# A two-layer MLP on one core: the second product in fp16 parts with ranges found on the way, three of four relu-squares split over two engines, and W2 read earlier

## The chip, the core and the metric

The kernel runs on one core of a Trainium2 chip. TensorE (PE in the profile, its weight loads PEld) multiplies, VectorE (DVE) and ScalarE (ACT) work element by element, GpSimd (POOL) does a few powers, and SyncE (SP) issues the DMA transfers from one queue, in order. The metric is the device time of one execution in microseconds; the median of several is compared.

## The reference

One layer of a hybrid backbone over 128 context tokens and 2048 latent tokens, with 1024 features. Each token stream goes through a mixer (gated DeltaNet beside a gated MLP over chunks), which the change doesn't touch, and then through this:

```python
h = rmsnorm(x, norm_ffn_l) * (1.0 + sc2) + sh2
x = x + ga2 * (jnp.square(jax.nn.relu(h @ w_ff1_l)) @ w_ff2_l)
...
y_prompt = rmsnorm(x, norm_final)
y_sample = rmsnorm(y, norm_final)
```

`w_ff1` is 1024 x 4096, `w_ff2` 4096 x 1024, all in fp32. Below, W1 and W2 are these two, z is the relu-square between them, and the gate is `ga2`. Latent and context tokens have gates and modulation of their own.

## The kernel before, in words

The program first makes the modulation, then the input projections with the mixer's first half, then the scans with the output projection, and last the MLP. Some 2500 us, of which the MLP is the second half.

**Parts.** An fp32 operand is multiplied as a high part and a low part: `mm3` (lines 309 to 315) makes three matmuls for each 128-wide piece of the contraction, high by high, high by low and low by high (lines 313, 314, 315). In the mixer and in the first MLP product the parts are fp16 (`split16x4`, line 1686: ScalarE writes the scaled high part, line 1694, VectorE the low part, line 1695). The scale is a power of two that is found from sums of squares of the operand: `powers` (line 223) turns a column of 128 maxima with a PE transpose (line 226), takes the largest on VectorE, spreads it over the partitions with a small PE product (line 231) and keeps the exponent. In the second MLP product the parts are `fp32r` (`split4`, line 1698: a ScalarE cast, line 1702, and a VectorE subtract, which has the line of `add`, 1684).

**First MLP product, 1201 to 1849 us.** The 2048 latent tokens times W1, in two halves of 1024 tokens and 16 pairs of 128-column blocks: 32 units (`Unit`). Each unit is a 2 x 2 block product done with seven products in place of eight (the numbers 1, 5, 6, 7, 3, 2, 4 are its steps, in that order), each of 12 matmuls of 512 columns. The moving operand (`hop`) is the normalised input in fp16 parts, the stationary one (`w`) sums or differences of W1 blocks, prepared six steps ahead. A unit's results are the four blocks of z: p (named for its first content, step 7), c12 (step 3), c11 (step 2) and c21 (step 4). VectorE adds up what PSUM holds (`add_scaled`, line 1707) and makes the relu-square in one instruction (`rl2`, line 1669); for c11 alone ScalarE does relu and square (lines 1803, 1804). Each block goes to DRAM (`z_d`, line 1765), and so do the sums s1 = c12 + p and s2 = s1 - c11 (line 1768), which the second product needs. The loop over the 224 steps (line 2116) sets the order in which all this is recorded, with other work between: `h2_steps` (the input of the second token half, first half of the loop), and `context_steps` (the same product for the 128 context tokens, second half). Also there, in the second half: the 16 differences of W2 blocks that the second product needs first, `sums_load(0, k)` at every sixth step and `sums(0, k)` four steps later (lines 2118 to 2122): two tiles r are loaded, VectorE subtracts them (line 1684), SP stores the result in `t_d`. A scheduling layer then moves instructions within each engine's queue by its own estimate of when their inputs are there.

**Second MLP product, 1849 to 2507 us.** Again seven products (1, 5, 6, 7, 3, 4, 2), each over eight or nine pairs of token tiles u and four quarters q of the contraction; one (product, u, q) is 12 matmuls of 512 columns. The stationary operand is z or a sum of its blocks (`s_load` reads it from DRAM five places ahead, `s_build` at line 1943 splits it three places ahead), the moving one the W2 blocks of the product (`t_build`, line 1885, four 128-row pairs to a `hop` buffer, four buffers to a product). `outcome` adds the PSUM results up, and `final` multiplies by the gate, adds the residual and normalises. Further differences of W2 are made during products 1, 5 and 6, and rows of the modulation during product 6.

**Buffers.** A pool of 49 tiles of 2 KB a partition (`wp`, line 170) holds all operands under way in the MLP: raw loads, split operands, blocks of z. A load waits until the tile it goes into has been given up. PSUM has eight banks (`bank`).

## Time and profile before

| | us |
|---|---|
| runs shown | 2512.78, 2520.37, 2521.24 |
| median | 2520.37 |
| the profiled execution's own time | 2515.55 |
| its span, first to last instruction | 2513.8 |
| first MLP product | 1201 to 1849 |
| second MLP product | 1849 to 2507 |

The clock granted to TensorE was 0.992 of full on average. A line of the profile such as `L313 PE MATMUL f<-hop,zH 128*128 128x512 f32 x944 | 367.3, 389 | 0.4 ...` reads: source line, engine, operation, output from inputs by the program's names, shape and type, count, then the busy time in us and the mean duration of one in ns, then the engine's idle time just ahead of these and what ended it. Matmuls overlap, so their pace is read from start to start and not from their durations. `SPq` is the queue of DMA issues.

### The profile page before, as it was taken

The numbers are of one execution on the slowest core, as the hardware profiler recorded it, in microseconds if no ns is written. First come the engines' busy times: TensorE is split into PE (matmuls) and PEld (weight loads), VectorE is DVE, ScalarE is ACT, GpSimd is POOL, SyncE is SP. The second block draws the span as 40 slices with busy tenths as digits, with TensorE's granted clock in tenths as the row PEclk, the third lists the DMA queues.
The fourth block names the chain that finished last, engine by engine and source line by source line (L and its number), as shares of the span: only waits on it lengthen the run. The fifth ranks groups of instructions, "written<-read, shape, count | busy, mean of one in ns | idle before, by whom it ended". The sixth has DMA issues, their size and how long they took to land.

```text
span 2513.8 us, 44098 instructions
## 1 busy us (share of the span) xinstructions
PE 2462.8 (98%) x15188; PEld 1666.3 (66%) x15188; DVE 1883.3 (75%) x3898; ACT 1339.5 (53%) x3257; POOL 236.9 (9%) x429
## 2 busy tenths in 40 slices
PE   8999999999999999999999999999999999999998
PEld 4666667666666787888444444444468888888887
DVE  4868886877778888986688988778765557685775
ACT  3756764566666667763456655445344323243442
POOL 3112222111111211110000000000000000000000
PEclk9999999999999999999999999999999999999999
DMA  8767755665656656774666778767689879776773
GB/s 293 227 179 216 221 164 174 201 202 183 205 186 194 203 169 216 250 239 134 218 205 205 232 233 283 242 206 221 188 282 315 312 251 334 239 263 200 236 255 108
DMA packets 482791, 558.23 MB, mean 222 GB/s; under 512 B 38068, under 2 KB 285148, under 8 KB 482566
## 3 DMA queue, kind: packets, MB, share of 16 engines
q1 hardware_dynamic: 482566, 555.41, 69.0%
q8 instruction: 119, 1.95, 0.3%
q14 instruction: 106, 0.87, 0.1%
HBM read 399.19 MB, written 156.08 MB: 221 GB/s over the span
## 4 chain that ended last, share of the span: by engine, by line
PE 78%; DVE 9%; DMA 6%; ACT 3%; issue 2%; SPq 1%; POOL 1%; POOLq 0%; DVEq 0%; ACTq 0%
PE f L315 15%; PE f L313 15%; PE f L314 15%; PE pj L313 5%; PE pj L314 5%; PE pj L315 5%; PE pd L1136 4%; PE pm L313 2%; PE pm L314 2%; PE pm L315 2%; DMA QK<-qk_d 2%; PE pt L683 1%; DMA r<-in_w_ff_dram 1%; DMA raw<-in_w_mod_dram 1%; PE pt L642 1%
## 5 line engine op out<-in xcount | busy, mean ns | idle before, releaser
L315 PE MATMUL f<-hop,zL 128*128 128x512 f32 (+1 forms) x976 | 376.2, 386 | 1.3 <-DVE zL L1684 1.2
L313 PE MATMUL f<-hop,zH 128*128 128x512 f32 (+1 forms) x976 | 376.4, 386 | 0.4 <-ACT zH L1702 0.4
L314 PE MATMUL f<-hop,zH 128*128 128x512 f32 (+1 forms) x976 | 376.1, 386 | 0.0
L313 PE MATMUL f<-hop,w 128*128 128x512 f16 x896 | 340.3, 381 | 3.1 <-ACT p L1786 2.3
L314 PE MATMUL f<-hop,w 128*128 128x512 f16 x896 | 341.1, 381 | 0.0
L315 PE MATMUL f<-hop,w 128*128 128x512 f16 x896 | 340.2, 381 | 0.0
L1702 ACT CAST zH<-zraw 128x512 fp32r<-128x512 f32 x240 | 146.4, 620 | 299.5 <-DMA zraw<-s_d 89.1
L314 PEld LDWEIGHTS <-w 128*128 128x128 f16 x1536 | 151.3, 99 | 148.8 <-issue 10.9
L313 PEld LDWEIGHTS <-w 128*128 128x128 f16 x1536 | 151.1, 98 | 146.9 <-issue 4.4
L315 PEld LDWEIGHTS <-w 128*128 128x128 f16 x1536 | 151.2, 98 | 146.5 <-issue 5.7
L1684 DVE TENSOR_TENSOR zL<-zraw,zH 128x512 fp32r<-128x512 f32 x240 | 163.2, 688 | 73.1 <-ACT zH L1702 58.5
L315 PEld LDWEIGHTS f<-hop,zL 128*128 128x128 f32 x976 | 183.4, 188 | 38.9 <-DVE zL L1684 2.2
L313 PEld LDWEIGHTS f<-hop,zH 128*128 128x128 f32 x976 | 183.4, 188 | 37.8 <-ACT zH L1702 0.9
L314 PEld LDWEIGHTS f<-hop,zH 128*128 128x128 f32 x976 | 183.4, 188 | 36.9 <-issue 0.2
L313 PE MATMUL pj<-kH,w 128*128 128x386 f16 (+2 forms) x568 | 180.3, 321 | 6.0 <-ACT w L205 3.3
L314 PE MATMUL pj<-kL,w 128*128 128x386 f16 (+2 forms) x568 | 181.2, 322 | 0.0
L315 PE MATMUL pj<-kH,w 128*128 128x386 f16 (+2 forms) x568 | 180.4, 321 | 0.0
L181 POOL TENSOR_TENSOR r<-rsq,nhalf 128x1 f32<-128x1 f32 (+1 forms) x37 | 27.7, 749 | 1368.2 <-DVE rsq L180 1368.2
L1694 ACT ACTIVATE w<-s,scales 128x512 f16<-128x512 f32 x96 | 68.7, 719 | 163.2 <-DVE s L1684 162.9
L1684 DVE TENSOR_TENSOR r<-r,r 128x512 f32<-128x512 f32 x64 | 44.2, 691 | 96.3 <-DMA r<-in_w_ff_dram 96.3
L629 DVE SCALAR_TENSOR_TENSOR cv<-pj,vec,cv 128x384 f32<-128x384 f32 (+2 forms) x142 | 83.1, 589 | 26.7 <-ACT cv L627 25.5
L313 PE MATMUL pj<-w,hrow 128*128 128x512 f16 x256 | 97.1, 379 | 0.1
(453 smaller groups left out, 5494.3 us busy)
## 6 DMA issues: line engine op xcount, KB each, us to landing
raw<-in_w_ff_dram SPq DMA_DIRECT2D x256, 256.0 KB
zraw<-z_d SPq DMA_DIRECT2D x212, 256.0 KB
z_d<-c SPq DMA_DIRECT2D x96, 256.0 KB
r<-in_w_ff_dram SPq DMA_DIRECT2D x96, 256.0 KB
zraw<-s_d SPq DMA_DIRECT2D x96, 256.0 KB
raw<-in_w_mod_dram SPq DMA_DIRECT2D x80, 256.0 KB
s_d<-s SPq DMA_DIRECT2D x64, 256.0 KB
t_d<-r SPq DMA_DIRECT2D x64, 256.0 KB
```

The source lines that it names most:

```text
L181: G.tensor_tensor(out=out, in0=t[:np_, :n], in1=nhalf[:np_, :n], op=ALU.pow)
L313: T.matmul(ps, lh, rh, start=first and i == 0, stop=False, skip_group_check=more)
L314: T.matmul(ps, lh, rl, start=False, stop=False, skip_group_check=more)
L315: T.matmul(ps, ll, rh, start=False, stop=last and i == n - 1, skip_group_check=more)
L629: V.scalar_tensor_tensor(out=cv, in0=ps[:, w : w + ncol - 2], scalar=convw[:, w, j : j + 1], in1=cv, op0=ALU.mult, op1=ALU.add)
L642: T.transpose(pq[:, i * P : (i + 1) * P], u["x2"][i], ident)
L683: T.matmul(ps[:, i * P : (i + 1) * P], kTt[:, i * P : (i + 1) * P], rhs[i], start=True, stop=True)
L1136: T.matmul(p[:, h, :], lhs[:, h, :], rhs[:, h, :], start=True, stop=True)
L1684: V.tensor_tensor(out=out, in0=a, in1=b, op=op)
L1694: A.activation(h, src, AF.Copy, scale=scale)
L1702: A.copy(h, src)
```

## The change

- z and W2 are split in fp16 parts, each scaled by a power of two; the product of the two scales is taken out again where the gate is multiplied in. Operand tiles take half the room: one pool tile in place of two for a piece of z, and two `hop` buffers in place of four for a product's W2.
- z's power comes from column sums of z itself (the squares of the relu), which ScalarE adds up while it squares (`accum_out`). So p, c12 and c21 become a max with 0 on VectorE and a square on ScalarE; c11 and the context tokens' squares get the sum too. `z_range` finds the power from the sums, for the first token half in the loop's second half, and for the others early in the second product.
- W2's power comes from squares of all of W2, which ScalarE makes (in place, 64 tiles). So the loop loads all four tiles of a step of W2, from step 11 on at every eleventh, and nine steps later subtracts two of them and squares all four. `w2_range` is recorded fifteen steps ahead of the first split of W2.
- A few of the steps of `h2_steps` move by one place.

Names in the rows below: p, c and s are the blocks and sums above, f is PSUM, w a split operand, r a tile of W2, `stats` the tile of column sums.

VectorE in one unit's steps 7 and 3, the program before:

```order
L1707 SCALAR_TENSOR_TENSOR c_21845<-f,scales,x 128x512 [waits DMAHW1_49,PE_49]
L1669 SCALAR_TENSOR_TENSOR p_21817<-p_21817 128x512 [waits DVE_49]
L1669 SCALAR_TENSOR_TENSOR c_21845<-c_21845 128x512 [waits DVE_49]
L1684 TENSOR_TENSOR s_21849<-c_21845,p_21817 128x512 [waits DVE_49]
L206 SCALAR_TENSOR_TENSOR w_21855<-raw,scales,w_21855 128x512 [waits DMAHW3_49,Activation_49]
L1695 SCALAR_TENSOR_TENSOR w_21861<-s,scales,w_21861 128x512 [waits Activation_49]
```

and with the change:

```order
L1737 SCALAR_TENSOR_TENSOR c_22079<-f,scales,x 128x512 [waits DMAHW2_49,PE_49]
L1681 TENSOR_SCALAR p_22050<-p_22050 128x512 [waits DVE_49]
L1681 TENSOR_SCALAR c_22079<-c_22079 128x512 [waits DVE_49]
L1722 TENSOR_TENSOR s_22084<-c_22079,p_22050 128x512 [waits Activation_49]
L1722 TENSOR_TENSOR t_22095<-r_21837,r_21835 128x512
L206 SCALAR_TENSOR_TENSOR w_22090<-raw,scales,w_22090 128x512 [waits DMAHW4_49,Activation_49]
```

The two relu-squares became two max, and the sum behind them now waits for ScalarE.

The SP queue around one read of W2 in the loop's second half, before:

```order
L1848 DMA z_d<-z_21586 256x1x128 [waits DMAHW2_49]
L1879 DMA r_21629<-in_w_ff_dram 128x512 [waits DMAHW3_49,PE_49]
L1879 DMA r_21631<-in_w_ff_dram 128x512 [waits DMAHW4_49]
L1905 DMA t_4_d<-r_21629 128x512 [waits DMAHW5_49,DVE_49]
L1765 DMA z_d<-p_21620 128x4x128 [waits DMAHW6_49,DVE_49]
```

and with the change, first on SP, then on ScalarE at the same place of the program:

```order
L1795 DMA z_d<-c_22118 128x4x128 [waits DMAHW3_49,Activation_49]
L187 DMA raw<-in_w_ff_dram 128x512 [waits DMAHW4_49,PE_49]
L1798 DMA s_d<-s_22122 128x4x128 [waits DMAHW5_49,DVE_49]
L1909 DMA r_22155<-in_w_ff_dram 128x512 [waits DMAHW6_49]
L1909 DMA r_22157<-in_w_ff_dram 128x512 [waits DMAHW7_49]
L1909 DMA r_22159<-in_w_ff_dram 128x512 [waits DMAHW0_49,PE_49]
L1909 DMA r_22161<-in_w_ff_dram 128x512 [waits DMAHW1_49,PE_49]
L1795 DMA z_d<-c_22145 128x4x128 [waits DMAHW2_49,Activation_49]
```

```order
L1677 ACTIVATE c_22145,stats<-c_22145 128x512 [waits DVE_49]
L1732 ACTIVATE w_22171<-raw,scales 128x512
L1805 ACTIVATE x<-f,scales 128x512 [waits DMAHW0_49,PE_49]
L1876 ACTIVATE z_22190,stats<-f 128x512 [waits PE_49]
L205 ACTIVATE w_22202<-raw,scales 128x512 [waits DMAHW3_49]
L1707 ACTIVATE r_22159,stats<-r_22159 128x512 [waits DMAHW0_49]
L1732 ACTIVATE w_22207<-raw,scales 128x512 [waits DMAHW7_49,DMAHW6_49]
L1809 ACTIVATE p_22223<-f,scales 128x512 [waits PE_49]
L1707 ACTIVATE r_22161,stats<-r_22161 128x512 [waits DMAHW1_49]
```

Before, the store of the difference stood directly behind its loads on SP. Now it stands far behind them, and so does the subtract on VectorE; but the squares of the two tiles that aren't subtracted stand on ScalarE about two steps behind the loads, in front of a copy out of PSUM (p).

The diff, cut to its core:

```diff
-    def rl2(out, src):
-        V.scalar_tensor_tensor(out=out, in0=src, scalar=0.0, in1=src, op0=ALU.max, op1=ALU.mult)
+    def square_z(c, g, n):
+        A.activation(c, c, AF.Square, accum_out=z_sums[g][:, n : n + 1])
+    def rl2(c, g, n):
+        V.tensor_scalar(out=c, in0=c, scalar1=0.0, scalar2=None, op0=ALU.max)
+        square_z(c, g, n)
+    def z_range(gs):
+        n, sl = len(gs), slice(gs[0], gs[-1] + 1)
+        top = smp.tile([P, 8], F32, tag="topc", name="topz", bufs=1)[:, 0:n]
+        for i, g in enumerate(gs):
+            V.tensor_reduce(out=top[:, i : i + 1], in_=z_sums[g], axis=mybir.AxisListType.X, op=ALU.max)
+        V.tensor_scalar_mul(top, top, 4.0)
+        powers(z_power[:, sl], z_under[:, sl], top, n, bank)
+        if 2 in gs:
+            V.tensor_scalar_mul(y_under, z_under, w2_under)
+    def w2_range():
+        top = smp.tile([P, 8], F32, tag="topc", name="topw", bufs=1)[:, 0:1]
+        V.tensor_reduce(out=top, in_=w2_sums, axis=mybir.AxisListType.X, op=ALU.max)
+        four_sum_power(w2_power, w2_under, top, bank, True)
+    def w2_loads(k):
+        return [fetch(rows2(k, h, n)) for h in (0, 1) for n in (0, 1)]
+    def w2_first(k, r):
+        d = w512("t5")
+        add(d, r[1], r[0], ALU.subtract)
+        store(out=t_d[5, k], in_=d)
+        for i in range(4):
+            A.activation(r[i], r[i], AF.Square, accum_out=w2_sums[:, 4 * k + i : 4 * k + i + 1])
...
     def t_build(raw, k):
-        if k % 4 == 0:
+        if k % 8 == 0:
             tcount.append(0)
-            moved.append(hop_tile(F32R, (len(tcount) - 1) % 5 < 2))
-        t = moved[-1][:, k % 4]
-        A.copy(t[:, 0, :], raw)
-        add(t[:, 1, :], raw, f32(t)[:, 0, :], ALU.subtract)
+            moved.append(hop_tile(F16, (len(tcount) - 1) % 5 < 2))
+        t = moved[-1][:, k % 8 // 4, k % 4]
+        raw = as4(raw)
+        A.activation(t[:, 0], raw, AF.Copy, scale=w2_power)
+        V.scalar_tensor_tensor(out=t[:, 1], in0=raw, scalar=w2_power, in1=t[:, 0], op0=ALU.mult, op1=ALU.subtract)
...
-    def s_build(raws, rest):
+    def s_build(raws, rest, u):
         if rest:
             add(raws[0], raws[0], raws[1], rest[0])
-        return split4(raws[0], "z")
+        g = token_group(u)
+        return split16x4(raws[0], z_power[:, g : g + 1])
...
-        add(y[n], y[n], ga[n], ALU.mult)
+        gated(y[n], y[n], ga[n], t)
...
-        if p > half + 7 and p % 6 == 0 and len(begun_sums) < NK:
+        if p >= 8 and p % 11 == 0 and len(begun_sums) < NK:
             begun_sums.append(p)
-            first_sums.append((p, len(begun_sums) - 1, sums_load(0, len(begun_sums) - 1)))
-        while first_sums and p >= first_sums[0][0] + 4:
-            sums(0, *first_sums.pop(0)[1:])
+            first_sums.append((p, len(begun_sums) - 1, w2_loads(len(begun_sums) - 1)))
+        while first_sums and p >= first_sums[0][0] + 9:
+            w2_first(*first_sums.pop(0)[1:])
+        if p == last - 12:
+            w2_range()
+        if p == half + 8:
+            z_range([0])
...
         us = products[n][1]
+        if m == 3:
+            z_range([1, 2])
```

More of the change, by code (lines that the diff above doesn't have):

```diff
@@ L1665, in hybrid_step @@
     wst.close()
-    def rl2(out, src):
-        V.scalar_tensor_tensor(out=out, in0=src, scalar=0.0, in1=src, op0=ALU.max, op1=ALU.mult)
+    stats = wp.tile([P, 512], F32, tag="w", name="stats")
+    z_sums = [stats[:, 0:64], stats[:, 64:128], stats[:, 128:136]]
+    w2_sums = stats[:, 192:256]
+    V.memset(stats[:, 256:384], 1.0)
+    phase["ones"] = stats[:, 256:384]
+    w2_power, w2_under = stats[:, 384:385], stats[:, 385:386]
+    z_power, z_under = stats[:, 386:389], stats[:, 389:392]
+    y_under = stats[:, 392:395]
+    def square_z(c, g, n):
[24 more added lines that the diff above has]
+            A.activation(r[i], r[i], AF.Square, accum_out=w2_sums[:, 4 * k + i : 4 * k + i + 1])
     hops["B"] = ctx.enter_context(tc.tile_pool(name="hopB", bufs=1, reuse_waits="tile"))
@@ L1695, in split16x4 @@
             V.scalar_tensor_tensor(out=lo, in0=src, scalar=scale, in1=h, op0=ALU.mult, op1=ALU.subtract)
-        return h, lo
-    def split4(src, name="w"):
-        h = wp.tile([P, 4, P], F32R, tag="w", name=name + "H")
-        lo = wp.tile([P, 4, P], F32R, tag="w", name=name + "L")
-        A.copy(h, src)
-        add(lo, src, f32(h), ALU.subtract)
         return h, lo
@@ L1788, in step @@
                 add(z, z, t["p5"])
-                rl2(z, z)
+                rl2(z, self.g, 4 * self.jp)
                 self.out(1, 1, z)
@@ L1794, in step @@
                 add_scaled(c, ps[5], t["x"])
-                rl2(c, c)
+                rl2(c, self.g, 4 * self.jp + 1)
                 self.out(0, 1, c)
@@ L1803, in step @@
                 A.activation(c, ps[1], AF.Relu, scale=mlp_under)
-                A.activation(c, c, AF.Square)
+                square_z(c, self.g, 4 * self.jp + 2)
                 self.out(0, 0, c)
@@ L1812, in step @@
                 add_scaled(c, ps[7], t["x"])
-                rl2(c, c)
+                rl2(c, self.g, 4 * self.jp + 3)
                 self.out(1, 0, c)
@@ L1902, in sums @@
     def sums(i, k, r):
-        if i < 2:
+        if i == 1:
             add(r[0], r[1], r[0], ALU.subtract)
-            store(out=t_d[7 if i else 5, k], in_=r[0])
+            store(out=t_d[7, k], in_=r[0])
         elif i == 5:
@@ L1958, in hybrid_step, with gated, half_out @@
     rows = {}
-    def half_out(y, n, x, ga, ss):
-        add(y[n], y[n], ga[n], ALU.mult)
+    def gated(out, y, ga, t):
+        g = 2 if t == 0 else 0 if t > 8 else 1
+        V.scalar_tensor_tensor(out=out, in0=y, scalar=y_under[:, g : g + 1], in1=ga, op0=ALU.mult, op1=ALU.mult)
+    def half_out(t, y, n, x, ga, ss):
+        gated(y[n], y[n], ga[n], t)
         add(y[n], y[n], x[n])
@@ L1970, in final @@
         ss = smp.tile([P, 2], F32, tag="ss2", name="ss2")
-        half_out(y, 1, x, ga, ss)
+        half_out(t, y, 1, x, ga, ss)
         def rest():
-            half_out(y, 0, x, ga, ss)
+            half_out(t, y, 0, x, ga, ss)
             r = smp.tile([P, 1], F32, tag="r", name="r")
@@ L1989, in final_last @@
         r = smp.tile([P, 1], F32, tag="r", name="r")
-        add(y[1], y[1], ga[1], ALU.mult)
+        gated(y[1], y[1], ga[1], t)
         add(y[1], y[1], x[1])
@@ L1993, in final_last @@
         add(y[1], y[1], nf[1], ALU.mult)
-        add(y[0], y[0], ga[0], ALU.mult)
+        gated(y[0], y[0], ga[0], t)
         add(y[0], y[0], x[0])
@@ L1999, in part @@
             c = slice(256 * h, 256 * h + 256)
-            add(x[0][:, c], ps[:, 0:256], ga[0][:, c], ALU.mult)
+            gated(x[0][:, c], ps[:, 0:256], ga[0][:, c], t)
             add(y[0][:, c], x[0][:, c], y[0][:, c])
@@ L2107, in hybrid_step @@
         p = 10 + 19 * j // 2
-        later += [(p + (-4, 0, 1, 2, 4, 5)[k] if k < 6 else p + 2 * k - 6, st[k]) for k in range(len(st))]
+        later += [(p + (-4, 0, 1, 2, 5, 6)[k] if k < 6 else p + 2 * k - 5, st[k]) for k in range(len(st))]
     later.sort(key=lambda e: e[0])
```

8 lines of the change are left out of this document (4 added, 4 removed).

## The prediction

> **What bounds the kernel now.** I read the page first, then the windows by stage, then the timeline of single matmuls, then the groups and the waits of the two MLP products. The page's first part has TensorE (PE) busy for nearly all of the span:
>
> ```profile
> PE 2462.8 (98%) x15188; PEld 1666.3 (66%) x15188; DVE 1883.3 (75%) x3898; ACT 1339.5 (53%) x3257; POOL 236.9 (9%) x429
> ```
>
> Busy says little of pace, so here is the busy time by stretch. The first MLP product runs from 1201 to 1849 us, the second from 1849 to 2507 us. Columns: stretch, its length, then busy time and instruction count of PE, weight loads, VectorE, ScalarE, GpSimd, then granted clock, DMA share, GB/s.
>
> ```profile
> 1200.00:1500.00 300.00, 296.84 (x1403) 139.20 (x1402) 246.16 (x403) 170.94 (x325) 8.18 (x9) 0.99 0.71 219
> 1700.00:1800.00 100.00, 98.36 (x462) 45.13 (x461) 79.59 (x123) 51.44 (x82) 0.00 (x0) 1.00 0.68 209
> 1900.00:2000.00 100.00, 100.00 (x443) 82.81 (x442) 51.03 (x78) 38.68 (x68) 0.00 (x0) 1.00 0.88 309
> ```
>
> At the same clock of 1.00 the first product issues 462 matmuls in 100 us, small gaps included, the second only 443, with none. The timeline of PE shows why: first two rows of the first product, then two of the second.
>
> ```profile
> 1700.18 0.38 PE L313 MATMUL f<-hop,w 128*128 128x512 f16 x1
> ...
> 1711.84 0.38 PE L313 MATMUL f<-hop,w 128*128 128x512 f16 x1
> ```
>
> ```profile
> 1929.69 0.39 PE L313 MATMUL f<-hop,zH 128*128 128x512 f32 x1
> ...
> 1935.81 0.39 PE L313 MATMUL f<-hop,zH 128*128 128x512 f32 x1
> ```
>
> Between the first pair lie 54 starts: 11.66 us / 54 = 215.9 ns from start to start. Between the second lie 27: 6.12 / 27 = 226.7 ns. The second product is bound by PE at 226.7 ns a matmul, the first at 215.9 ns plus a few stalls. The groups carry the counts:
>
> ```profile
> L313 PE MATMUL f<-hop,zH 128*128 128x512 f32 x944 | 367.3, 389 | 0.4 <-ACT zH L1702 0.4
> L313 PEld LDWEIGHTS f<-hop,zH 128*128 128x128 f32 x976 | 183.4, 188 | 37.8 <-ACT zH L1702 0.9 <-issue 0.2
> L313 PEld LDWEIGHTS <-w 128*128 128x128 f16 x149 | 14.6, 98 | 17.4
> L1684 DVE TENSOR_TENSOR zL<-zraw,zH 128x512 fp32r<-128x512 f32 x240 | 163.2, 688 | 73.1 <-ACT zH L1702 58.5 <-PE f L314 4.6 <-issue 2.7
> L1702 ACT CAST zH<-zraw 128x512 fp32r<-128x512 f32 x240 | 146.4, 620 | 299.5 <-DMA zraw<-s_d 89.1 <-DVE zraw L1684 84.5 <-DMA zraw<-z_d 71.6
> L1695 DVE SCALAR_TENSOR_TENSOR w<-raw,scales,w 128x512 f16<-128x512 f32 x14 | 10.2, 743 | 0.0
> L1694 ACT ACTIVATE w<-raw,scales 128x512 f16<-128x512 f32 x14 | 9.9, 714 | 0.0
> L341 DVE TENSOR_SCALAR macc<-mraw,scond 128x512 f32<-128x512 f32 x4 | 1.7, 479 | 0.0
> L1669 DVE SCALAR_TENSOR_TENSOR c<-c 128x512 f32<-128x512 f32 x12 | 8.2, 686 | 0.1
> ```
>
> **The second product in fp16.** Its 3 x 944 = 2832 full matmuls (three lines of equal count) go from fp32r to fp16. No row of this kernel has an fp16 stationary z. Bounds: nothing gained (226.7 ns stays) or the whole step to 215.9 ns. I take the second, since the first product's row has the same shape, the same three-part sum and the same 98 ns weight load that the change will have in place of 188 ns. 2832 x 10.8 ns = **30.6 us**; the 96 half-width matmuls add some 0.5 us at most. Sum **-31 us**, all on the path, as PE has no gap in that stage that would swallow it.
>
> What pays for it: each of 240 + 112 splits becomes a scaled copy and a subtract. ScalarE +0.1 us each (714 against 620 ns), VectorE +0.055 us (743 against 688): 35 and 19 us over 658 us. Cover: VectorE was busy 51 of 100 us and ScalarE 39 there; in the fullest 20 us below VectorE has 18.3, which the extra 0.055 in 0.69 and the faster pace bring near 20. With no cover, 19 us would be lost.
>
> **The relu-squares.** Three of four per unit (32 units) were one VectorE instruction of 686 ns; now they are a max (nearest rows: 479 ns single-source, 686 at worst; I take 479) and a square on ScalarE with a column sum. That pair's price on ScalarE is in the timeline of the same form, L972, 0.61 us from start to start:
>
> ```profile
> 1360.27 0.62 ACT L972 ACTIVATE junk<-x 128x512 f32<-128x512 f32 x1
> 1360.79 0.19 ACT L972 ACTIVATION_READ_ACCUMULATOR junk<-x 128x1 f32 x1
> 1360.88 0.62 ACT L972 ACTIVATE junk<-x 128x512 f32<-128x512 f32 x1
> ```
>
> A new wait appears: s1 = c12 + z22 stands on VectorE right behind the two max, and now waits for two squares on ScalarE. Free ScalarE: 0.6 to 1.3 us; I take 1.0. Queued behind it on VectorE are the low halves of the next weights and the c21 sum, for which PE waits. Per unit of 300 / 16 = 18.7 us VectorE had 18% = 3.4 us idle (first window); it gains 3 x 0.2 us, and pays 1.0 of wait and 0.69 x 7/11 = 0.4 for the W2 difference that now falls in this half: +0.8 us, inside the 3.4. ScalarE: 57% busy; 3 x 0.61 plus 4 x 0.61 x 7/11 for W2 is 3.4 us of 18.7: 75%. I take **+2 us** of small stalls for it (0 if all fit).
>
> **W2 earlier.** In the second half of the first product, waits and the traces of one stall:
>
> ```profile
> DVE r L1684 <- DMA r<-in_w_ff_dram: 53.0, 13, 5.6
> ACT w L1694 <- DVE s L1684: 158.0, 55, 8.2
> PE f L1845 <- ACT r L1840: 3.2, 3, 1.9
> PE f L313 <- ACT p L1786: 2.3, 1, 2.3
> ```
>
> ```profile
> SPq L1905 <- DVE r L1684: 41.4, 10, 8.2
> ```
>
> ```profile
> 1652.72 0.69 DVE L1684 TENSOR_TENSOR r<-r,r 128x512 f32<-128x512 f32 x1 [5.23 <-DMA r<-in_w_ff_dram]
> ```
>
> ```profile
> 1654.71 0.72 ACT L1694 ACTIVATE w<-s,scales 128x512 f16<-128x512 f32 x1 [7.39 <-DVE s L1684]
> 1655.34 0.67 ACT L1786 ACTIVATE p<-f,scales 128x512 f32<-128x512 f32 x1
> ```
>
> ```profile
> 1653.40 0.38 PE L315 MATMUL f<-hop,w 128*128 128x512 f16 x1
> 1656.06 0.38 PE L313 MATMUL f<-hop,w 128*128 128x512 f16 x1 [2.29 <-ACT p L1786]
> ...
> 1656.94 0.63 PE L314 MATMUL f<-hop,w 128*128 128x512 f16 x1
> ...
> 1660.33 0.38 PE L313 MATMUL f<-w,w 128*128 128x512 f16 x1
> ```
>
> VectorE waits 5.2 us for a W2 tile that came late; ScalarE waits 7.4 us for a weight sum queued behind it; a PSUM copy (p) queued behind that holds PE for 2.3 us. After the gap eight matmuls take 3.39 us (1656.94 to 1660.33) in place of 1.73: the stall costs 2.3 + 1.7. The SP queue stood too, on the store of that difference. The change puts the subtract a unit or more behind its load, so PE's 2.3 and 3.2 us with two slow tails (1.7 shown, the other estimated alike) should go: 5.5 + 3.4 = **-9 us**. What is late next: two of the four squares of W2 stand on ScalarE only two steps (5 to 6 us) behind their load, with PSUM copies behind them, so some of that wait moves to ScalarE. I leave **+3 us** of it.
>
> The clock row can be set against the Trainium skill, page "TensorE: Matmul & The Clock Gate", section "HAM oscillation": gaps under about 3.4 us should not slow the clock. The trace disagrees, as a gap of 2.66 us did. By the rule the credit would be 5.5 us and the total some 3 us higher; the row decides.
>
> **The range tests.** Three power computations add a transpose and a small product on PE, amid other matmuls. The same helper's row (min, median, max ns):
>
> ```profile
> L226 PE MATMUL pm<-ident,topw x2: 270/272/273, 797.8 to 807.4; 128*1 128x128 f32 x2
> ```
>
> Three such pieces apiece, overlapped or not: 1 to 2.4 us together; **+1 us**. The stores' wait on SP lengthens by the square; SP gains the 41.4 us above, so nothing is added. The gate's multiply gets a scalar (743 against 688 ns), off PE's path but for two half tiles at the end: 0.1 us.
>
> **DMA in the second product.** Same bytes in less time:
>
> ```profile
> 1860.00:1880.00 20.00, 18.32 (x80) 14.57 (x79) 8.91 (x13) 5.93 (x10) 0.00 (x0) 1.00 1.02 357
> 1880.00:1900.00 20.00, 20.00 (x90) 16.53 (x89) 10.21 (x15) 6.08 (x10) 0.00 (x0) 1.00 0.98 338
> 1900.00:1920.00 20.00, 20.00 (x90) 16.57 (x89) 9.20 (x15) 6.43 (x11) 0.00 (x0) 1.00 0.94 316
> 1920.00:1940.00 20.00, 20.00 (x90) 16.57 (x89) 10.55 (x17) 10.50 (x19) 0.00 (x0) 1.00 1.00 358
> ...
> 2120.00:2140.00 20.00, 19.91 (x88) 16.16 (x88) 18.32 (x30) 10.38 (x18) 0.00 (x0) 1.00 1.04 377
> ```
>
> 1860 to 1940 moves 342 GB/s on average; at the new pace the demand is 342 x 226.7 / 215.9 = 359. The trace reached 377 for 20 us, so it just fits: **+2 us**.
>
> Sum: -31 + 2 - 9 + 3 + 1 + 2 = **-32 us**. The profiled execution took 2515.55 us (span 2513.8): 2483.5. The median shown is 2520.37, the runs lie between 2512.78 and 2521.24, so a median may stand up to 5 us above that sum; I say **2484 us**.
>
> **Rivals.**
> A. *The DMA engines become the bound in the first three products.* For: the shares of 0.94 to 1.04 above. Against: 377 GB/s was reached, and a z operand now takes one buffer, not two, so loads can run further ahead. If 1849 to 2150 kept its old pace, 300 x 4.8% = 14 us are lost: **2498**. The Trainium skill, page "DMA: Bandwidth & Descriptors", section "Where 436 GB/s comes from", puts the limit of one core at HBM at some 358 GB/s. By that rule the 359 above is at the limit; the row of 377 passes it.
> B. *W2's wait moves to ScalarE whole, and the kernel gets slower.* Place: the squares two steps behind their load, in front of PSUM copies, and now also in the first half, where VectorE has the least idle time. Price of one event: 2.3 + 1.7 = 4 us of PE, as at 1653. 16 batches x 4 = 64 against the 31 + 9 gained: slower by some 24 us, **2540**. It decides from 10 events on; from 13 on it is over 0.5%. Against: of 13 VectorE waits for W2, of up to 5.6 us, four PE waits at most came (rows above), and ScalarE has 43% idle. With four events more: about **2500**.
> C. *fp16 brings no pace* with z stationary: 2515.5 - 9 + 6 = **2512**. Against: the pace and the weight loads (98, 188 ns) go with the operand type in the rows above.
>
> **How the numbers follow.** Forecast 0.71; A 0.12; B in part 0.10, whole 0.04; C 0.03. A measurement of this kernel tells about 0.5% (12.6 us) from no change: below 2507.8 is faster. Forecast, A and two thirds of B in part (the other third 2507 and up) give faster 0.90; that third, and C, give same 0.06; B whole gives slower 0.04. Range: below, every stall gone and none new (2515.5 - 31 - 9 = 2475.5) less the 3 us by which runs fall under the profiled one, and a little for stalls that I did not list: 2469. Above, A plus 5 us of run offset: 2503. Outside are most of B and C.
>
> **What would show it.** Right: matmuls of the second product 216 ns apart, its stage some 628 us long in place of 658, weight loads near 98 ns; the VectorE wait for W2 near nothing and no stall of 2 us behind it; small VectorE waits of about 1 us at s1. Wrong: a pace above 220 ns (C); PE waiting for z operands with DMA share at 1 (A); ScalarE's squares waiting for W2, with PE waiting for PSUM copies (B).

## The result, and the profile after

The changed kernel takes 2506.73 us (median of 11 runs) against 2520.31 us for the kernel before (11 runs): a ratio of **0.9943, 95% interval 0.9931 to 0.9956**. It is faster by 0.6%; the prediction said 2484 us, 1.4% faster, and its range ended at 2503. The profiled execution has a span of 2505.0 us.

The table splits the span by the timeline of PE: from the first matmul of the first MLP product to its 1344th of 2688 ("first half"), from there to the first matmul of the second product ("second half"), and from there to its last matmul. The kernels after the second row are the experiments; a * marks those that leave a search for a power out. One of e3's four runs took 2783.97 us, in a slower state of the chip (granted clock 0.849), and is left out of its median.

| kernel | first half | second half | second product | median, us | ratio to before, 95% interval |
|---|---|---|---|---|---|
| before | 304.6 | 342.9 | 657.7 | 2520.31 | |
| after | 329.7 | 342.2 | 627.9 | 2506.73 | 0.9943 (0.9931 to 0.9956) |
| e1_late | 313.2 | 337.3 | 628.0 | 2484.28 | 0.9863 (0.9849 to 0.9878) |
| e2_now2 * | 303.2 | 333.3 | 631.8 | 2473.18 | 0.9820 (0.9803 to 0.9836) |
| e3_noz * | 320.1 | 339.9 | 624.6 | 2493.41 | 0.9905 (0.9889 to 0.9922) |
| e4_const * | 300.8 | 334.9 | 626.7 | 2467.51 | 0.9798 (0.9783 to 0.9812) |
| e5_before_early | 315.5 | 334.9 | 656.0 | 2518.32 | 0.9999 (0.9986 to 1.0011) |
| e6_spread | 312.9 | 333.7 | 626.8 | 2482.28 | 0.9861 (0.9846 to 0.9875) |
| e7_spread_defer | 312.4 | 334.4 | 626.2 | 2481.85 | 0.9858 (0.9843 to 0.9873) |
| e9_fp16_alone * | 300.3 | 332.6 | 626.7 | 2463.41 | 0.9788 (0.9767 to 0.9809) |
| e10_half2 | 301.4 | 339.2 | 629.0 | 2477.25 | 0.9841 (0.9818 to 0.9863) |
| e11_before_own | 302.9 | 332.5 | 655.8 | 2500.20 | 0.9934 (0.9913 to 0.9955) |
| e12_pool | 345.4 | 357.8 | 627.5 | 2537.55 | 1.0079 (1.0057 to 1.0102) |
| e13_room | 303.0 | 346.2 | 628.5 | 2485.79 | 0.9880 (0.9862 to 0.9897) |

The time until the first product starts, in which none of the kernels differs by an edit, lies between 1194 and 1205 us; differences of a few us in the whole are therefore read from the stages.

So the second product gave 29.8 us, as forecast, and the **first half of the first product took 25.1 us back**. The page's first part and the windows by stage, in the columns of the prediction:

```profile
PE 2429.4 (97%) x15197; PEld 1406.7 (56%) x15197; DVE 1882.2 (75%) x3923; ACT 1472.3 (59%) x3617; POOL 232.9 (9%) x430
```

```profile
1200.00:1500.00 300.00, 277.61 (x1292) 128.14 (x1291) 219.71 (x377) 202.76 (x461) 5.73 (x9) 0.98 0.73 228
1700.00:1800.00 100.00, 100.00 (x471) 46.15 (x470) 78.86 (x130) 68.70 (x140) 0.00 (x0) 1.00 0.72 213
1900.00:2000.00 100.00, 100.00 (x465) 45.33 (x464) 54.35 (x79) 43.80 (x69) 0.00 (x0) 1.00 0.86 306
```

From 1900 to 2000 PE now issues 465 matmuls, before 443. From 1700 to 1800 it issues 471 in place of 462. From 1200 to 1500 it issues 1292 in place of 1403, though neither VectorE nor ScalarE is full there: VectorE went from 246 to 220 us of busy time and ScalarE from 171 to 203. The pace of the second product, in the timeline of PE:

```profile
1929.29 0.38 PE L313 MATMUL f<-hop,w 128*128 128x512 f16 x1
...
1935.12 0.38 PE L313 MATMUL f<-hop,w 128*128 128x512 f16 x1
```

27 starts lie between these rows: 5.83 us / 27 = 215.9 ns. The groups, each shape apart, give the durations that the prediction took from neighbours:

```profile
L313 PEld LDWEIGHTS <-w 128*128 128x128 f16 x2512 | 246.4, 98 | 263.0 <-ACT w L1732 5.1 <-issue 4.7 <-ACT w L205 3.8
L1677 ACT ACTIVATE c<-c 128x512 f32<-128x512 f32 x96 | 60.1, 626 | 41.9 <-DVE c L1681 40.8
L1707 ACT ACTIVATE r<-r 128x512 f32<-128x512 f32 x64 | 39.9, 625 | 56.3 <-DMA r<-in_w_ff_dram 51.0 <-DVE t L1722 4.9
L1681 DVE TENSOR_SCALAR c<-c 128x512 f32<-128x512 f32 x64 | 26.7, 419 | 0.2
L1722 DVE TENSOR_TENSOR s<-c,p 128x512 f32<-128x512 f32 x32 | 22.1, 691 | 33.0 <-ACT c L1677 26.9 <-ACT p L1677 6.1
```

Weight loads take 98 ns; the max takes 419 ns where 479 was taken; z's squares (L1677) and W2's (L1707) take 0.63 us. The third row holds the loss: 56.3 us of ScalarE's idle time lie just before W2's 64 squares, 51.0 of them for the read of W2. The waits over both halves of the first product (total, times, longest) say what it was paid with:

```profile
ACT r L1707 <- DMA r<-in_w_ff_dram: 51.0, 16, 6.0
PE f L313 <- ACT x L1805: 16.1, 6, 7.2
PE f L313 <- ACT p L1809: 3.3, 2, 2.7
PE f L313 <- ACT p L1816: 3.1, 2, 2.2
PE f L992 <- DVE x L985: 5.1, 3, 2.5
```

Before, VectorE waited for r 53.0 us in 13 waits. The wait is as long as it was; it only changed engine, and it now comes once for every one of the 16 batches. PE waits 22.5 us for PSUM copies (x and p) in place of 2.3. The last row is PE waiting to transpose the input of the second token half (`h2_steps`), 5.1 us in place of 2.4. One stall on a PSUM copy, on both engines, first PE, then ScalarE:

```profile
1302.29 0.38 PE L315 MATMUL f<-hop,w 128*128 128x512 f16 x1
1309.85 0.59 PE L313 MATMUL f<-hop,w 128*128 128x512 f16 x1 [7.17 <-ACT x L1805]
1310.22 0.63 PE L314 MATMUL f<-hop,w 128*128 128x512 f16 x1
...
1315.34 0.48 PE L314 MATMUL f<-hop,w 128*128 128x512 f16 x1
```

```profile
1300.79 1.49 ACT L995 ACTIVATE ev<-f,b,a 128x128 f32<-128x128 f32 x4
1305.28 0.63 ACT L1707 ACTIVATE r<-r 128x512 f32<-128x512 f32 x1 [3.00 <-DMA r<-in_w_ff_dram]
...
1305.90 0.61 ACT L1707 ACTIVATE r<-r 128x512 f32<-128x512 f32 x1
...
1306.52 0.61 ACT L1677 ACTIVATE c<-c 128x512 f32<-128x512 f32 x1
...
1307.13 0.71 ACT L1732 ACTIVATE w<-raw,scales 128x512 f16<-128x512 f32 x1
1307.74 1.48 ACT L995 ACTIVATE ev<-f,b,a 128x128 f32<-128x128 f32 x4
1309.11 0.69 ACT L1805 ACTIVATE x<-f,scales 128x512 f32<-128x512 f32 x1
```

ScalarE stands 3.0 us at a square whose W2 tile has not landed. That square, a second one, a z square, a weight cast and four copies of h2 then run ahead of the PSUM copy x, for which PE stands 7.2 us. The twelve starts from 1310.22 to 1315.34 are 427 ns apart, not 216. Taking every pair of starts more than 0.24 us apart, less 0.216 us each, the first half has 29.1 us of such excess after (3.9 before), the second 8.7 (10.1 before). Ten of the pairs are over 1.2 us apart, eight in the first half; the 37.8 us come to 3.8 us for each of the ten, slow tails and the shorter pairs included. Three of the ten (1.6, 2.9 and 1.7 us) are waits for the h2 input and not for a PSUM copy. Without W2's squares (e2, below) no pair in the whole first product is over 1.2 us apart.

### The profile page after: what moved, and what is told of

It reads as the page before. It is cut to its first block, busy times and chain, and to the rows that moved or that the text cites. A ratio compares the mean times of both kernels' runs of the same rounds, so it can differ in the third digit from the quotient of the medians.

```text
span 2505.0 us, 44544 instructions
## 1 busy us (share of the span) xinstructions
PE 2429.4 (97%) x15197; PEld 1406.7 (56%) x15197; DVE 1882.2 (75%) x3923; ACT 1472.3 (59%) x3617; POOL 232.9 (9%) x430
## 4 chain that ended last, share of the span: by engine, by line
PE 69%; DVE 11%; DMA 9%; ACT 6%; issue 2%; SPq 1%; POOL 1%; POOLq 0%; DVEq 0%; ACTq 0%
PE f L313 12%; PE f L315 12%; PE f L314 12%; PE pj L313 5%; PE pj L314 5%; PE pj L315 5%; PE pd L1136 4%; DMA QK<-qk_d 2%; PE pm L313 2%; PE pm L314 2%; PE pm L315 2%; DMA r<-in_w_ff_dram 2%; DVE w L1733 1%; PE pt L683 1%; ACT w L1732 1%
## 5 line engine op out<-in xcount | busy, mean ns | idle before, releaser
L313 PE MATMUL f<-hop,w 128*128 128x512 f16 (+1 forms) x1872 | 707.5, 379 | 24.2 <-ACT x L1805 16.1
L314 PE MATMUL f<-hop,w 128*128 128x512 f16 (+1 forms) x1872 | 708.3, 378 | 0.0
L315 PE MATMUL f<-hop,w 128*128 128x512 f16 (+1 forms) x1872 | 706.8, 378 | 0.9 <-DVE w L1733 0.9
L314 PEld LDWEIGHTS <-w 128*128 128x128 f16 x2512 | 246.5, 98 | 279.3 <-issue 31.5
L313 PEld LDWEIGHTS <-w 128*128 128x128 f16 x2512 | 246.4, 98 | 263.0 <-ACT w L1732 5.1
L315 PEld LDWEIGHTS <-w 128*128 128x128 f16 x2512 | 246.3, 98 | 258.3 <-issue 3.4
L1732 ACT ACTIVATE w<-zraw,stats 128x512 f16<-128x512 f32 x240 | 168.4, 718 | 253.1 <-DVE zraw L1722 78.4
L1733 DVE SCALAR_TENSOR_TENSOR w<-zraw,stats,w 128x512 f16<-128x512 f32 x240 | 176.7, 746 | 57.5 <-ACT w L1732 57.4
L1733 DVE SCALAR_TENSOR_TENSOR w<-s,scales,w 128x512 f16<-128x512 f32 x96 | 71.7, 749 | 42.5 <-ACT w L1732 42.1
L629 DVE SCALAR_TENSOR_TENSOR cv<-pj,vec,cv 128x384 f32<-128x384 f32 (+2 forms) x142 | 83.0, 589 | 25.3 <-ACT cv L627 24.1
L313 PE MATMUL pj<-w,hrow 128*128 128x512 f16 x256 | 97.1, 379 | 0.1
L315 PE MATMUL pj<-w,hrow 128*128 128x512 f16 x256 | 97.0, 379 | 0.0
L314 PE MATMUL pj<-w,hrow 128*128 128x512 f16 x256 | 97.0, 379 | 0.0
L1921 ACT ACTIVATE hop<-traw,stats 128x512 f16<-128x512 f32 x112 | 75.9, 712 | 26.4 <-DMA traw<-in_w_ff_dram 17.6
L1922 DVE SCALAR_TENSOR_TENSOR hop<-traw,stats,hop 128x512 f16<-128x512 f32 x112 | 79.9, 745 | 14.7 <-ACT hop L1921 14.6
L206 DVE SCALAR_TENSOR_TENSOR w<-raw,scales,w 128x512 f16<-128x512 f32 x112 | 81.8, 743 | 11.0 <-ACT w L205 11.0
L313 PE MATMUL pm<-wH,oH 128*128 128x512 f32 x208 | 88.1, 424 | 0.5 <-DVE tmp L1529 0.3
```

What stands on the lines that cost most here:

```text
L206: V.scalar_tensor_tensor(out=t[:, 1, :], in0=raw, scalar=scale, in1=t[:, 0, :], op0=ALU.mult, op1=ALU.subtract)
L313: T.matmul(ps, lh, rh, start=first and i == 0, stop=False, skip_group_check=more)
L314: T.matmul(ps, lh, rl, start=False, stop=False, skip_group_check=more)
L315: T.matmul(ps, ll, rh, start=False, stop=last and i == n - 1, skip_group_check=more)
L629: V.scalar_tensor_tensor(out=cv, in0=ps[:, w : w + ncol - 2], scalar=convw[:, w, j : j + 1], in1=cv, op0=ALU.mult, op1=ALU.add)
L1732: A.activation(h, src, AF.Copy, scale=scale)
```

## Experiments

The theories: **W**, the loss is the place of W2's squares on ScalarE, close behind their load; **L**, it is the amount of added work in a half that has little room; **Q**, what remains after W is the place of other queue entries; **Z**, it is z's squares and the waits that they bring.

**e1_late: W2's squares later.** The four squares of a batch may not run on ScalarE before the last ScalarE work of the step before the difference, nine steps behind the load; nothing else changes.

```diff
+        start = here()
         for i in range(4):
             A.activation(r[i], r[i], AF.Square, accum_out=w2_sums[...])
+        behind("acts", start, (mybir.EngineType.Activation,))
...
+        new = [x for x in instructions[start:] if x.engine == mybir.EngineType.Activation]
+        done["acts"] = new or done.get("acts", [])
```

> The four squares of each step of W2 are held on ScalarE behind the copies and squares of the step ahead of which they are recorded, nine steps behind their load; nothing else changes. In the changed kernel the first half of the first MLP product takes 329.7 us (304.6 before), the second 342.2 (342.9). Theory W (ScalarE waits for W2 tiles that it meets two steps behind their load, with PSUM copies queued behind): the nine ScalarE waits of 26.4 us in the first half go, it takes 308 to 315 us, the second half some 337, the whole 15 to 22 us less than the changed kernel (about 2488). Theory Z (z's squares and the waits between VectorE and ScalarE that they bring): the first half stays at 326 or more, the whole within 5 us of 2507. Theory L (ScalarE simply has more to do, wherever it stands): as Z.

Measured 2484.28 us, 22.4 us under the changed kernel. In the waits of the first product, ScalarE's row for r and the DMA is gone, and PE's rows shrink to these:

```profile
PE f L313 <- ACT x L1807: 6.0, 3, 4.8
PE f L313 <- ACT p L1818: 1.5, 1, 1.5
```

The first half takes 313.2 us, 16.5 less, with the same squares on the same engine, as W expected. It is not back at 304.6: W carries most of the loss, not all.

**e2_now2, e3_noz, e4_const: the searches left out.** e2 leaves out W2's squares and their test (power fixed at 8192); e3 leaves out z's column sums and test (power fixed at 0.125) and returns to one VectorE instruction for the relu-square; e4 leaves out both.

```diff
 e2:
-            A.activation(r[i], r[i], AF.Square, accum_out=w2_sums[...])
-        four_sum_power(w2_power, w2_under, top, bank, True)
+        V.memset(w2_power, 8192.0)
 e3:
-        V.tensor_scalar(out=c, in0=c, scalar1=0.0, scalar2=None, op0=ALU.max)
-        square_z(c, g, n)
+        V.scalar_tensor_tensor(out=c, in0=c, scalar=0.0, in1=c, op0=ALU.max, op1=ALU.mult)
-        powers(z_power[:, sl], z_under[:, sl], top, n, bank)
+        V.memset(z_power[:, sl], 0.125)
```

> Leaves out the squares of W2 and the search for its power, which is set to the constant 8192; the loads and the difference stay. Theory W: first half 305 to 312 us, whole about 2485; a little better than with the squares held back, as 64 x 0.6 us of ScalarE go too. Theory Z: first half 322 or more. Theory L: about half of the 25 us come back, first half 315 to 320, and clearly better than with the squares held back.

> Leaves out z's column sums and the search for its power, which is set to the constant 0.125; the relu-square is one VectorE instruction again, and W2's squares stay as in the changed kernel. Theory Z: first half 305 to 312 us, whole about 2487. Theory W: the nine waits for W2 on ScalarE stay, first half 320 or more, whole within 8 us of 2507. Theory L: half of it back, 315 to 320.

> Leaves out both searches (z's power 0.125, W2's 8192, no squares of W2, no column sums, one VectorE instruction for the relu-square): fp16 parts and early reads of W2 alone. All theories: first half 300 to 306 us, second half 335 (my credit of 9 us for the earlier subtract, which the changed kernel did not show, with no wait for W2 left), second product 628, whole 2470 to 2480. If the second half stays at 342, the credit was wrong and not merely eaten up by ScalarE's waits.

Measured 2473.18, 2493.41 and 2467.51 us. Without W2's squares the first half is 303.2 us: they cost 26.5 us there and 8.9 in the second half (342.2 to 333.3). z's search costs 13.3 us by the medians beside W2's squares (after to e3; 9.6 us by the two ratios to the kernel before) and 5.7 without them (e2 to e4). Each theory missed something here: e2 came out 12 us below the 2485 that W gave; e3's first half is as W said, but its whole lies more than W's 8 us below the changed kernel, so z's squares carry a part; L's 315 to 320 us for the first half is far off in e2 and just missed in e3. e4's stages are as expected, its whole 2.5 us below the range. Windows of one stretch of the first half, of e2 and of the changed kernel:

```profile
1210.00:1500.00 290.00, 288.35 (x1367) 134.61 (x1366) 236.28 (x407) 193.77 (x421) 5.77 (x9) 1.00 0.81 253
```

```profile
1210.00:1500.00 290.00, 267.61 (x1246) 123.58 (x1244) 217.37 (x374) 197.46 (x453) 5.73 (x9) 0.98 0.72 223
```

ScalarE is as busy in the fast one (193.8 of 290 us) as in the slow one (197.5), and DMA moves more. A busy share does not tell these two apart; the wait in the queue does.

**e5_before_early: the early read alone.** The kernel before, in fp32r, with W2 read from step 11 on, every 11th step, and subtracted nine steps behind.

```diff
-        if p > half + 7 and p % 6 == 0 and len(begun_sums) < NK:
+        if p >= 8 and p % 11 == 0 and len(begun_sums) < NK:
-        while first_sums and p >= first_sums[0][0] + 4:
+        while first_sums and p >= first_sums[0][0] + 9:
```

> The kernel before, with one change alone: the two W2 tiles of each first difference are loaded from step 11 on at every eleventh and subtracted nine steps later (fp32r parts and one-instruction relu-squares stay, no squares of W2). My prediction gave this part 9 us. If that holds by itself: second half of the first MLP product 334 to 337 us (342.9 before), first half 303 to 308, second product 658, whole 2508 to 2512. If the scheduling layer moves the subtract close behind its load again: no gain, 2516 to 2520, with VectorE waits for these tiles now in both halves.

Measured 2518.32 us, ratio 0.9999: nothing. The second half gained 8.0 us and the first lost 10.9. Its waits over the first product, and the longest of them, some 7 us ahead of PE's longest gap there (4.4 us, until 1318.39):

```profile
DVE r L1684 <- DMA r<-in_w_ff_dram: 47.4, 14, 6.4
```

```profile
1307.39 0.69 DVE L1684 TENSOR_TENSOR r<-r,r 128x512 f32<-128x512 f32 x1 [6.36 <-DMA r<-in_w_ff_dram]
```

The difference was asked for nine steps behind its load, yet in the order that runs it stands 1.5 to 3 steps (a step is 12 matmuls, 2.6 us) behind it, so the wait went along into the first half. To ask for a later step is not what makes it late enough.

**e11_before_own: a tile of its own.** The kernel before with the difference written to another tile and not over one of its operands; steps as before.

```diff
-            add(r[0], r[1], r[0], ALU.subtract)
-            store(out=t_d[7 if i else 5, k], in_=r[0])
+            d = w512("t5") if i == 0 else r[0]
+            add(d, r[1], r[0], ALU.subtract)
+            store(out=t_d[7 if i else 5, k], in_=d)
```

> The kernel before, with one edit: W2's first difference goes into a tile of its own in place of one of its two operands; reads, step numbers and fp32r as before. Theory D, the stalls of the second half were the price of the difference standing 4 to 5 us behind its load, and a tile of its own lets it stand 10 us or more behind, as in e9_fp16_alone: the waits of VectorE for r (53.0 us, 13) are gone, the second half takes 332 to 334 us in place of 342.9, median 2508 to 2511. Rival, the second half of e9_fp16_alone (332.6) was short because of other parts of the change (the weights' splits, the searches left out), not because of the wait: 341 to 344 and a median of 2516 to 2520.

Measured 2500.20 us, ratio 0.9934, better than expected (2508 to 2511): this one edit, without fp16, gives as much as the whole change. The waits over the first product and a window of its second half:

```profile
DVE t L1684 <- DMA r<-in_w_ff_dram: 2.5, 1, 2.5
```

```profile
1500.00:1800.00 300.00, 300.00 (x1408) 138.18 (x1406) 251.38 (x384) 159.49 (x252) 0.00 (x0) 1.00 0.78 240
```

Of the 53.0 us of waits 2.5 remain for the first difference, and the second half takes 332.5 us in place of 342.9, with no gap of PE in it. So the stalls that the prediction priced at 9 us are worth 10.4, and they go by placing the difference further behind its load (6 to 16 us behind the issue of its first load, 12 of the 16 over 10 us; 4.5 to 8.5 us before), whatever is done about fp16. Why the median fell by more, 18 to 20 us, isn't settled: the span fell 15.3, of which 1.3 lie ahead of the first product, 1.7 in its first half and 1.9 in the second product.

**e9_fp16_alone: the second product alone.** The changed kernel with both searches left out (powers fixed), one-instruction relu-squares, and W2's first differences read at the steps of the kernel before, two tiles at a time, into a tile of their own.

```diff
-    return [fetch(rows2(k, h, n)) for h in (0, 1) for n in (0, 1)]
+    return [fetch(rows2(k, 0, n)) for n in (0, 1)]
-        if p >= 8 and p % 11 == 0 and len(begun_sums) < NK:
+        if p > half + 7 and p % 6 == 0 and len(begun_sums) < NK:
-        while first_sums and p >= first_sums[0][0] + 9:
+        while first_sums and p >= first_sums[0][0] + 4:
 (and the edits of e2_now2 and e3_noz)
```

> fp16 parts alone: leaves out both searches (z's power 0.125, W2's 8192), one-instruction relu-squares, and W2's first differences read as before (every sixth step of the second half, subtracted four steps later). Second product 625 to 630 us as in all with fp16, first half 300 to 306. If the earlier read is worth 8 us (334.9 against 342.9 in the second half), the second half is 341 to 345 here and the whole 2474 to 2479, against 2467.5 with the earlier read; if it is worth nothing, 335 and 2466 to 2470.

Measured 2463.41 us, ratio 0.9788. The second product takes 626.7 us (31.0 less), the second half 332.6 as in e11, and in the whole first product no two starts of PE are more than 0.24 us apart:

```profile
1210.00:1500.00 290.00, 290.00 (x1381) 136.24 (x1379) 246.50 (x404) 167.51 (x321) 7.97 (x9) 1.00 0.72 218
1500.00:1800.00 300.00, 300.00 (x1407) 138.20 (x1406) 249.99 (x381) 156.45 (x248) 0.00 (x0) 1.00 0.78 241
```

The 341 to 345 us that were expected if the earlier read were worth 8 us did not come: the second half is short with the reads where they were, since the difference has a tile of its own here, as in e11. Against this kernel the changed one loses 29.4 us in the first half and 9.6 in the second: 39 us for the two searches and the reads that W2's search needs.

**e6_spread, e7_spread_defer: other places.** e6 puts one square of W2 in each step, from six steps behind the load, and the difference eight behind. e7 also holds the last z square of a unit (c21) and its store behind the copies of the next step.

```diff
 e6:
+        if first_sums and p == first_sums[0][0] + 6:
+            w2_later.extend((first_sums[0][1], i, first_sums[0][2][i]) for i in (2, 3))
+        while first_sums and p >= first_sums[0][0] + 8:
             w2_first(*first_sums.pop(0)[1:])
+        if w2_later:
+            w2_square()
 e7:
-                rl2(c, self.g, 4 * self.jp + 3)
-                self.out(1, 0, c)
+                V.tensor_scalar(out=c, in0=c, scalar1=0.0, scalar2=None, op0=ALU.max)
+                put_off.append(rest)
```

> The changed kernel with the squares of W2 recorded one to a step, from six steps behind their load on (the difference eight steps behind), each held on ScalarE behind the step ahead; with all four together held nine steps behind it ran 2484.3 us, first half 313.2. Theory Q (what is left is the place in ScalarE's queue: four squares in a row, 2.4 us, in front of a weight split and a PSUM copy): first half 305 to 309, whole 2474 to 2479, near the 2473.2 without any squares of W2. Theory L (what is left is ScalarE's amount of work): first half 311 to 315, whole 2482 to 2486, as with the four in a row.

> As the one with W2's squares one to a step, and the square of c21 with its store held back behind the copies of the following step, so that it no longer stands in front of the next unit's first PSUM copy (x). Theory Q: another 2 to 5 us less, whole 2470 to 2475. Theory L: no change against the one without this. If the later store makes the sums or the second product wait: 2 to 6 us more.

Measured 2482.28 and 2481.85 us. In e6 the second half is clean (333.7 against 333.3 without any W2 square), but the first stays at 312.9; e7 changes nothing that can be told. Q falls. What is left of W2's squares is some 10 us, all in the first half; what holds it there was only tried by moving the reads, next.

**e10_half2, e13_room: other steps.** Both keep e6's spreading. e10 moves all 16 batches into the second half (every fifth step), e13 starts 16 steps before the middle (every sixth).

```diff
-        if p >= 8 and p % 11 == 0 and len(begun_sums) < NK:
+        if p >= half + 3 and p % 5 == 0 and len(begun_sums) < NK:      (e10)
+        if p >= half - 16 and p % 6 == 0 and len(begun_sums) < NK:     (e13)
-        if p == last - 12:
+        if p == last - 5:
             w2_range()
```

> The kernel after, with the squares of W2 spread one per step as in e6_spread (difference eight steps behind the load), and all 16 reads moved into the second half of the first product (every fifth step there). Nothing is left out. Theory L, the first half has no room on ScalarE and VectorE for 28 more squares and 7 differences, the second half has: first half 302 to 304 us as in e2_now2 (303.2), second half 334 to 337, median 2470 to 2475. Rival, the amount of squares costs the same wherever it stands: first half 303, second half 343 or more, median 2480 to 2484, as e6_spread (2482.28).

> The kernel after, with W2's squares spread as in e6_spread and the 16 reads on every sixth step from 16 steps before the middle of the first product, where its other work (the h2 transposes and their copies) has nearly ended. Nothing is left out. Theory L, what a batch costs depends on the room beside it: 7 batches in the full first half cost 11 us (e6_spread 312.9 against 301.4 in e10_half2), 16 in the second half 6 us (339.2 against 333.7 with 9), so a rate in between costs 2 to 4 us: first half 301 to 304, second 335 to 337, median 2472 to 2476. Rival, the six us of the second half in e10_half2 come from having all squares there at any rate: 339 or more and a median of 2477 or more.

e10 measured 2477.25 us, ratio 0.9841: the fastest that keeps both searches, though its interval overlaps those of e6 and e7. The first half is 301.4, as L says; the second is 339.2, between L's 337 and the rival's 343, so 16 batches do cost there, some 6 us. e13 missed: 2485.79 us. Its first half is 303.0, but the second 346.2, with a stall of a new kind. Two windows just after the middle and PE's wait, of e13, then a window of e10 around the same time:

```profile
1500.00:1520.00 20.00, 20.00 (x95) 9.04 (x94) 18.35 (x32) 16.25 (x35) 0.00 (x0) 1.00 1.06 365
1520.00:1540.00 20.00, 16.23 (x65) 7.10 (x64) 8.48 (x13) 9.74 (x22) 0.00 (x0) 0.83 1.07 364
```

```profile
1530.61 0.58 PE L313 MATMUL f<-hop,w 128*128 128x512 f16 x1 [3.77 <-DMA hop<-hop_d]
```

```profile
1520.00:1540.00 20.00, 20.00 (x97) 9.38 (x95) 14.07 (x29) 10.64 (x25) 0.00 (x0) 1.00 1.06 362
```

In e13 an operand of the second half (hop) comes late, and PE pays 3.8 us and a slow clock (0.83). The DMA share alone doesn't explain it: it is over 1 in e10 too, where PE has no gap. What differs is the order on SP. In e13 four reads of W2 go out at 1501.7 to 1507.4 us, ahead of the last four hop reads, which go out from 1523.4 on; in e10 no read of W2 stands there, and these hop reads go out from 1518.8 on. That this order is the cause was not tried apart. If so, "room" is not one quantity: beside ScalarE's queue the DMA queue of that stretch counts. Two more gaps of 2.1 us in e13 are waits for the copy x; what sets them was not tried.

**e12_pool: W2's squares on GpSimd.**

```diff
-            A.activation(r[i], r[i], AF.Square, accum_out=w2_sums[...])
+            tc.nc.gpsimd.tensor_tensor(out=r[i], in0=r[i], in1=r[i], op=ALU.mult)
+            tc.nc.gpsimd.tensor_tensor(out=w2_most, in0=w2_most, in1=r[i], op=ALU.add)
```

> The kernel after, with W2's squares on GpSimd in place of ScalarE: each of the 64 tiles is multiplied by itself and added to one tile of sums (128 instructions of 128x512), whose largest entry gives the power. Nothing is left out. No row shows such an instruction on GpSimd; the nearest take 647 to 726 ns (128x512, one input), so 83 us at least of 640, on an engine that is busy 8 us in 300. Theory S, the loss is ScalarE's time and queue alone: first half 303, second half 333, median 2471 to 2476, as e2_now2 (2473.18). Rival, GpSimd's work slows VectorE beside it (its 128x512 add over 690 ns): first half above 312, median above 2482.

Measured 2537.55 us, slower than before by 0.8%, and in both halves slower than the changed kernel, as the rival said. The groups from 1198 to 1500 us, of e12 and then of the changed kernel:

```profile
L1711 POOL TENSOR_TENSOR most<-most,r 128x512 f32<-128x512 f32 x28 | 44.0, 1573 | 1.3
L1710 POOL TENSOR_TENSOR r<-r 128x512 f32<-128x512 f32 x30 | 38.7, 1305 | 124.8 <-DVE t L1726 45.7 <-DMA r<-in_w_ff_dram 19.0 <-DMA raw<-in_w_ff_dram 16.1
L1737 DVE SCALAR_TENSOR_TENSOR w<-raw,scales,w 128x512 f16<-128x512 f32 x42 | 38.1, 914 | 3.8 <-ACT w L1736 3.8
L1741 DVE SCALAR_TENSOR_TENSOR c<-f,scales,x 128x512 f32<-128x512 f32 x27 | 20.0, 744 | 0.7 <-PE f L315 0.6
L1681 DVE TENSOR_SCALAR c<-c 128x512 f32<-128x512 f32 x26 | 12.5, 484 | 0.1
```

```profile
L1733 DVE SCALAR_TENSOR_TENSOR w<-raw,scales,w 128x512 f16<-128x512 f32 x42 | 31.0, 745 | 8.7 <-ACT w L1732 8.7
L1737 DVE SCALAR_TENSOR_TENSOR c<-f,scales,x 128x512 f32<-128x512 f32 x27 | 20.0, 744 | 0.8 <-PE f L315 0.8
L1681 DVE TENSOR_SCALAR c<-c 128x512 f32<-128x512 f32 x27 | 11.3, 419 | 0.1
```

The same VectorE instruction with two SBUF inputs takes 914 ns in place of 745 on average, and the max of c with one input 484 in place of 419; the one that takes its first input from PSUM (f) stays at 744. GpSimd's 128x512 instructions take 1.3 to 1.6 us. The engine that looked free slows VectorE, and the first half takes 345.4 us. But the slow VectorE is not the only cause in sight. GpSimd now waits for W2 as well, and the powers that h2's input needs (line 181) stand in the same queue; PE's waits for that input went from 5.1 to 12.9 us:

```profile
POOL r L1710 <- DMA r<-in_w_ff_dram: 40.8, 10, 12.3
PE f L992 <- DVE x L985: 12.9, 5, 3.7
```

How the loss divides between the two was not tried.

## Why the prediction was wrong

- **The second product (-31 us): right.** 627.9 us where 628 was forecast, 215.9 ns a matmul; 31.0 us in e9. Rival C fell. Rival A fell too: in the whole stage only six pairs of starts are over 0.24 us apart, 4.7 us together, and the longest (2.8 us) is a range test, below. The 96 half-width matmuls gave 1.1 us where 0.5 at most was allowed (120 ns from start to start before, 109 after).
- **The stalls of the second half (-9 us): the size right, the reason incomplete.** e11 gives 10.4 us for it; in the changed kernel W2's squares took 8.9 us of it back, so the second half gained only 0.7. But the credit was given to the earlier read; e5 shows that the early read in the form of the kernel before only moves the wait, and e11 that a tile of its own is enough without it.
- **What is late next (+3 us): this step failed.** It saw that two of four squares stand close behind their load, with PSUM copies behind them, and then left 3 us for it. W2's squares cost 35.4 us (after against e2: 26.5 and 8.9); spread over later steps 25.3 of these go (after against e6: 16.8 and 8.5). The mechanism is **rival B**, with a side path that B did not name (three of the ten gaps come by way of h2's input). B's price of 4 us for an event came out at 3.8, in part by luck: one gap of 7.55 us makes up for seven that had no slow tail. What was wrong is the number of events: ten of 16 batches, where the 3 us stood for less than one. The argument against it, that 13 VectorE waits had cost PE four at most, does not carry over: VectorE's queue held mostly weight parts, which are made six steps ahead, ScalarE's holds PSUM copies, for which PE waits within a step. (That this is why more of the waits reached PE is argued from the order and the rows above; no run tried it apart.) "In part" (four events more, 2500, with a chance of 0.10) was the nearest case and still too few, and the range stopped at A's 2498 plus 5 us.
- **The relu-squares (+2 us) and the range tests (+1 us): too small, a lesser error.** Between e9 and e2, which differ by z's search and the form of the W2 reads, the first product grows by 3.6 us and the second by 5.1; between e4 and e2, by z's search alone, the medians differ by 5.7. Part of it is the test itself, for which PE stands at the start of the second product:

```profile
1887.10 0.38 PE L231 MATMUL f<-topd,stats 2*128 2x2 f32 x2 [2.42 <-DVE topd L230]
```

 The share of 75% that this step worked out for ScalarE came out at 68% (203 of 300 us), because a unit grew from 19.0 to 20.6 us; the work per unit was as reckoned, and it was not what decided.
- **DMA in the second product (+2 us): as forecast within the error**, as 657.7 less 30.6 is 627.1 and 627.9 came out.
- **The sum:** -29.8 in the second product, +25.1 and -0.7 in the two halves of the first and -3.5 ahead of them are, but for rounding, the 8.8 us by which the span fell (2513.8 to 2505.0). The last is in work that the change doesn't touch.

## What to carry to other kernels

A wait that is moved is not removed: price it by what is queued behind it on the new engine and by how soon that is needed, and take one event for each batch as the upper end of the range until a row says otherwise (here 16 events of 4 us, 64 us; 35 came, and 3 were forecast). Put work that only has to be done some time, such as sums for a range test, several steps behind its load and one instruction at a time; that gave 22 to 24 us here (e1, e6), nearly as much as fp16. And before a change of precision is credited with a clean stage, try the small edit alone: one tile of its own for a difference gave 0.7%.
